# Mean of ReLU over rows: a rearranged tail, scaling on GpSimd, and a first load issued ahead of the entry barrier

## The chip, the core and the metric

The kernel runs on one core of a Trainium2 chip. The core has five engines with instruction streams of their own: TensorE (not used here), VectorE (DVE in the profile), ScalarE (ACT), GpSimd (POOL) and SyncE (SP). SyncE computes nothing; here it issues all DMA transfers. [...] The metric is the device time of one execution, in microseconds (us); smaller is better.

## The reference

```python
batch, seq, dim = 32, 512, 1024
x = np.random.randn(batch, seq, dim).astype(np.float32)

def reference(x):
    relu_x = np.maximum(x, 0)
    return np.mean(relu_x, axis=-1).astype(np.float32)
```

16384 rows of 1024 floats, 67.1 MB in all, are read once; 16384 floats (64 KB) are written.

## The kernel before, in words

The 16384 rows are laid out over 128 partitions, 128 rows to a partition (`J` = 128), so that row j of a partition is one column of a 128x128 result. The input is read in tiles of 16 rows to a partition (`NB` = 16, 8 MB), through a pool of three buffers. The first seven tiles are loaded whole, each with one DMA on SyncE's queue (L79). The last tile is loaded in pieces that get smaller (`row_pieces` 8, 4, 2, 1 rows, L86; then the sixteenth row in `col_pieces` of 512, 256 and 256 columns, L90), so that little is left to compute when the last byte lands. A load into a used buffer waits until VectorE and ScalarE are done with that buffer's rows.

A row is one instruction: it takes the maximum with zero and sums along the row into one column. Odd rows go to VectorE (`dve_row`, L20, sums in `sum_v`), even rows to ScalarE (`act_row`, L15, sums in `sum_a`). Each such instruction is followed by a short one that reads the accumulator out (`DVE_READ_ACCUMULATOR`, `ACTIVATION_READ_ACCUMULATOR`).

`finish` (L71) multiplies finished sums by 1/1024 into `res`: VectorE the odd columns (L73), ScalarE the even ones (L74). It is called twice: for the 112 columns of the first seven tiles, and for 14 columns of the last tile.

Rows 14 and 15 of the last tile are the tail (L101 to L119):

- row 14, whole: ScalarE sums its first 512 columns, VectorE its last 512; VectorE adds the halves and scales (L106);
- row 15, columns 0 to 511: ScalarE sums 256, VectorE 256;
- row 15, columns 512 to 767: VectorE; then VectorE adds the three parts so far (L111);
- row 15, columns 768 to 1023: VectorE; then VectorE adds and scales (L116);
- the store of `res` (L120) waits for L116.

Before all this stands an entry barrier of all five engines (L135 in the profile): each engine signals, GpSimd collects the signals after it has filled four constants, and releases all. The program's order on each engine is the order in which the code issues its instructions; semaphores are placed by the framework.

Of the kernel before, what the change touches and what calls it, by code (L numbers as in the profile page):

```python
# [1 line left out]

# [4 lines left out]

F32 = mybir.dt.float32
ALU = mybir.AluOpType
RELU = mybir.ActivationFunctionType.Relu  # L10


def act_row(nc, src, acc):

    nc.scalar.activation(out=src, in_=src, func=RELU, accum_out=acc)  # L15


def dve_row(nc, src, acc):

    nc.vector.tensor_scalar(  # L20
        out=src, in0=src, scalar1=0.0, scalar2=None,
        op0=ALU.max, op1=ALU.add, accum_out=acc,
    )


@with_exitstack
def kernel(
    ctx: ExitStack,
    tc: tile.TileContext,
    x: bass.AP,  # L30
    out: bass.AP,
):
    nc = tc.nc
    P = nc.NUM_PARTITIONS
    xf = x.flatten_outer_dims()
    R, D = xf.shape
    assert R % P == 0
    J = R // P
    inv = 1.0 / D
    xr = xf.rearrange("(p j) d -> p j d", p=P, j=J)  # L40
    outr = out.flatten().rearrange("(p j) -> p j", p=P, j=J)

    NB = 16
    BUFS = 3
    full = J // NB - 1

    row_pieces = []
    left = NB
    while left > 1:
        row_pieces.append(left // 2)  # L50
        left -= left // 2
    col_pieces = [D // 2, D // 4, D // 4]

    in_pool = ctx.enter_context(tc.tile_pool(name="in", bufs=BUFS))
    res_pool = ctx.enter_context(tc.tile_pool(name="res", bufs=1))
    sum_a = res_pool.tile([P, J], F32)
    sum_v = res_pool.tile([P, J], F32)
    res = res_pool.tile([P, J], F32)
    part_a = res_pool.tile([P, 2], F32)
    part_v = res_pool.tile([P, 4], F32)  # L60

    def rows(xt, lo, n, j0):

        for k in range(lo, lo + n):
            j = j0 + k
            if j % 2:
                dve_row(nc, xt[:, k, :], sum_v[:, j:j + 1])
            else:
                act_row(nc, xt[:, k, :], sum_a[:, j:j + 1])

    def finish(lo, hi):  # L71

        nc.vector.tensor_scalar_mul(out=res[:, lo + 1:hi:2], in0=sum_v[:, lo + 1:hi:2], scalar1=inv)  # L73
        nc.scalar.mul(out=res[:, lo:hi:2], in_=sum_a[:, lo:hi:2], mul=inv)  # L74

    for t in range(full):
        j0 = t * NB
        xt = in_pool.tile([P, NB, D], F32, name="xt")
        nc.sync.dma_start(out=xt, in_=xr[:, j0:j0 + NB, :])  # L79
        rows(xt, 0, NB, j0)  # L80

    j0 = full * NB
    xt = in_pool.tile([P, NB, D], F32, name="xt")
    lo = 0
    for n in row_pieces:
        nc.sync.dma_start(out=xt[:, lo:lo + n, :], in_=xr[:, j0 + lo:j0 + lo + n, :])  # L86
        lo += n
    c = 0
    for w in col_pieces:
        nc.sync.dma_start(out=xt[:, lo, c:c + w], in_=xr[:, j0 + lo, c:c + w])  # L90
        c += w

    finish(0, j0)
    lo = 0
    for n in row_pieces[:-1]:
        rows(xt, lo, n, j0)
        lo += n
    finish(j0, j0 + lo)


    last = xt[:, NB - 1, :]  # L101
    act_row(nc, xt[:, lo, :D // 2], part_a[:, 0:1])
    dve_row(nc, xt[:, lo, D // 2:], part_v[:, 0:1])
    act_row(nc, last[:, :D // 4], part_a[:, 1:2])
    dve_row(nc, last[:, D // 4:D // 2], part_v[:, 1:2])
    nc.vector.tensor_scalar(  # L106
        out=res[:, J - 2:J - 1], in0=part_a[:, 0:1], scalar1=part_v[:, 0:1], scalar2=inv,
        op0=ALU.add, op1=ALU.mult,
    )
    dve_row(nc, last[:, D // 2:3 * D // 4], part_v[:, 2:3])  # L110
    nc.vector.tensor_scalar(  # L111
        out=part_v[:, 1:2], in0=part_v[:, 1:2], scalar1=part_a[:, 1:2], scalar2=part_v[:, 2:3],
        op0=ALU.add, op1=ALU.add,
    )
    dve_row(nc, last[:, 3 * D // 4:], part_v[:, 3:4])
    nc.vector.tensor_scalar(  # L116
        out=res[:, J - 1:J], in0=part_v[:, 3:4], scalar1=part_v[:, 1:2], scalar2=inv,
        op0=ALU.add, op1=ALU.mult,
    )  # L119
    nc.sync.dma_start(out=outr, in_=res)  # L120


# [1 line left out]
_INS = ['x']  # L124
_OUTS = [((32, 512), 'float32')]


# [23 lines left out]
```

## Time and profile before

| what | us |
|---|---|
| median of 10 runs (164.80 to 165.31) | 164.93 |
| the profiled execution, its own time | 164.94 |
| span of it, first to last instruction | 163.2 |
| VectorE busy | 75.4 |
| ScalarE busy | 69.5 |
| GpSimd busy | 0.2 |
| first load issued at | 0.73 |
| store issued at | 160.74 |

Times in the profile count from the span's start. In a timeline row the columns are start, duration, engine, line, operation, tiles and shapes; what stands in square brackets is how long the engine had been idle and what released it. `SPq` is SyncE's own queue. A DMA row of the chain of waits runs from issue to landing.

### The profile page before, as it was taken

What the parts mean: (1) busy time and instruction counts of PE and PEld (TensorE: products, weight loads), DVE (VectorE), ACT (ScalarE), POOL (GpSimd) and SP (SyncE); (2) the same over time, 40 slices, a digit from 0 to 9 for tenths busy, and PEclk for the clock granted to TensorE, in tenths of its full rate; (3) what the DMA queues carried; (4) which work ended last, traced back from release to release, by engine and by line L of the source; (5) the groups of instructions that cost most, each with busy time, mean ns of one, the idle gap of its engine ahead of it and who ended that gap; (6) DMA issues with size and microseconds to landing.
All of it is one profiled execution on the core that took longest, in us unless ns stands there. A gap on an engine that the chain in (4) does not pass through costs nothing.

```text
span 163.2 us, 351 instructions
## 1 busy us (share of the span) xinstructions
DVE 75.4 (46%) x139; ACT 69.5 (43%) x133; POOL 0.2 (0%) x4
## 2 busy tenths in 40 slices
DVE  0000039800696008930099202990049700799993
ACT  3000039600694008910099002980059500797890
POOL 0000000000000000000000000000000000000000
DMA  7989998998997996996997998998999898999970
GB/s 257 514 353 418 514 418 353 514 418 353 514 450 321 514 482 289 514 482 289 514 498 325 466 482 353 450 514 370 402 514 402 370 514 353 418 442 398 412 291 16
DMA packets 2162, 67.19 MB, mean 412 GB/s; under 512 B 240, under 2 KB 624, under 8 KB 880
## 3 DMA queue, kind: packets, MB, share of 16 engines
q1 hardware_dynamic: 2160, 67.18, 96.0%
q14 instruction: 2, 0.02, 0.0%
HBM read 67.11 MB, written 0.07 MB: 412 GB/s over the span
## 4 chain that ended last, share of the span: by engine, by line
DMA 83%; DVE 14%; SPq 1%; issue 0%; DVEq 0%
DMA xt<-in_x_dram 83%; DVE xt L20 13%; SPq L86 0%; SPq L79 0%; DVE part_v L111 0%; DVE res L116 0%; DVE res L106 0%; DVE res L73 0%; DVEq L20 0%; DVEq L111 0%; DVEq L106 0%
## 5 line engine op out<-in xcount | busy, mean ns | idle before, releaser
L20 DVE TENSOR_SCALAR_CACHE_REDUCE xt<-xt 128x1024 f32<-128x1024 f32 (+1 forms) x67 | 74.4, 1172 | 85.0 <-DMA xt<-in_x_dram 84.9
L15 ACT ACTIVATE xt<-xt 128x1024 f32<-128x1024 f32 (+1 forms) x65 | 66.8, 1028 | 88.9 <-DMA xt<-in_x_dram 88.9
L15 ACT ACTIVATION_READ_ACCUMULATOR xt<-xt 128x1 f32 x65 | 12.2, 188 | 0.0
L20 DVE DVE_READ_ACCUMULATOR xt<-xt 128x1 f32 x67 | 5.6, 83 | 0.0
L15 ACT ACT_TABLE_LOAD x1 | 1.3, 1283 | 0.7 <-PEq L135 0.7
L74 ACT ACTIVATE res<-sum_a 128x56 f32<-128x56 f32 (+1 forms) x2 | 0.5, 235 | 0.1
L73 DVE TENSOR_SCALAR res<-sum_v 128x56 f32<-128x56 f32 (+1 forms) x2 | 0.4, 184 | 0.1
L111 DVE TENSOR_SCALAR part_v<-part_v,part_a 128x1 f32<-128x1 f32 x1 | 0.3, 272 | 0.1
L106 DVE TENSOR_SCALAR res<-part_a,part_v 128x1 f32<-128x1 f32 x1 | 0.2, 214 | 0.1
L116 DVE TENSOR_SCALAR res<-part_v 128x1 f32<-128x1 f32 x1 | 0.2, 215 | 0.0
L135 POOL MEMSET const-bfloat16-1.0<- 128x1 bf16 x1 | 0.1, 101 | 0.0
L135 POOL MEMSET const-uint8-127<- 128x1 uint8 x1 | 0.1, 101 | 0.0
L135 POOL MEMSET const-float32-0.0<- 128x1 f32 x1 | 0.1, 98 | 0.2 <-issue 0.2
L135 POOL MEMSET const-float32-1.0<- 128x1 f32 x1 | 0.1, 98 | 0.0
## 6 DMA issues: line engine op xcount, KB each, us to landing
xt<-in_x_dram SPq DMA_DIRECT2D x1, 4096.0 KB, 39.0
xt<-in_x_dram SPq DMA_DIRECT2D x1, 2048.0 KB, 43.5
xt<-in_x_dram SPq DMA_DIRECT2D x1, 1024.0 KB, 45.5
xt<-in_x_dram SPq DMA_DIRECT2D x1, 512.0 KB, 46.4
xt<-in_x_dram SPq DMA_DIRECT2D x1, 256.0 KB, 46.5
xt<-in_x_dram SPq DMA_DIRECT2D x2, 128.0 KB, 42.7
xt<-in_x_dram SPq DMA_DIRECT2D x7, 49.1
out_dram<-res SPq DMA_DIRECT2D x1, 64.0 KB, 1.5
```

Source lines behind the costliest of these rows:

```text
L15: nc.scalar.activation(out=src, in_=src, func=RELU, accum_out=acc)
L20: nc.vector.tensor_scalar(out=src, in0=src, scalar1=0.0, scalar2=None, op0=ALU.max, op1=ALU.add, accum_out=acc,)
L73: nc.vector.tensor_scalar_mul(out=res[:, lo + 1:hi:2], in0=sum_v[:, lo + 1:hi:2], scalar1=inv)
L74: nc.scalar.mul(out=res[:, lo:hi:2], in_=sum_a[:, lo:hi:2], mul=inv)
L106: nc.vector.tensor_scalar(out=res[:, J - 2:J - 1], in0=part_a[:, 0:1], scalar1=part_v[:, 0:1], scalar2=inv, op0=ALU.add, op1=ALU.mult,)
L111: nc.vector.tensor_scalar(out=part_v[:, 1:2], in0=part_v[:, 1:2], scalar1=part_a[:, 1:2], scalar2=part_v[:, 2:3], op0=ALU.add, op1=ALU.add,)
L116: nc.vector.tensor_scalar(out=res[:, J - 1:J], in0=part_v[:, 3:4], scalar1=part_v[:, 1:2], scalar2=inv, op0=ALU.add, op1=ALU.mult,)
L135: nc = _bacc.Bacc("TRN2", target_bir_lowering=False, num_devices=1)
```

## The change

Five things are done.

1. All sums go to one tile `sums`. `finish` becomes one GpSimd instruction over all columns, odd and even, in place of one on VectorE and one on ScalarE.
2. Row 14's halves are added and scaled on GpSimd.
3. Row 15: ScalarE also takes 128 of the columns 512 to 767, VectorE the other 128. VectorE's instructions for row 15 start from the sum of the one before (`init`, an operand in SBUF), so that no add is needed between them. GpSimd scales ScalarE's first part; ScalarE multiplies its second part by 1/1024 and adds that; VectorE's last instruction scales its running sum and adds ScalarE's.
4. The store waits for VectorE and for GpSimd's third instruction.
5. After the program has been compiled, its first load (the first tile, 8 MB) is taken out of the body and put ahead of SyncE's drain in the entry barrier. The other loads stay behind the barrier.

The built program differs in one more instruction: at the start of GpSimd's body, behind the barrier, stands a request to load a library of GpSimd instructions, which the program before does not have.

```diff
-def dve_row(nc, src, acc):
+def dve_row(nc, src, acc, init=None):
     nc.vector.tensor_scalar(
-        out=src, in0=src, scalar1=0.0, scalar2=None,
+        out=src, in0=src, scalar1=0.0, scalar2=init,
         op0=ALU.max, op1=ALU.add, accum_out=acc,
     )
+def issue_ahead_of_entry_barrier(nc):
+    entry, body = nc.cur_f.blocks[0].instructions, None
...
+    first = body[load]
...
+    del body[load]
+    at = next(k for k, i in enumerate(entry) if i.engine == first.engine and i.opcode == "Drain")
+    entry.insert(at, first)
...
     def finish(lo, hi):
-        nc.vector.tensor_scalar_mul(out=res[:, lo + 1:hi:2], in0=sum_v[:, lo + 1:hi:2], scalar1=inv)
-        nc.scalar.mul(out=res[:, lo:hi:2], in_=sum_a[:, lo:hi:2], mul=inv)
+        nc.gpsimd.tensor_scalar(
+            out=res[:, lo:hi], in0=sums[:, lo:hi], scalar1=inv, scalar2=0.0, op0=ALU.mult, op1=ALU.add,
+        )
...
-    act_row(nc, xt[:, lo, :D // 2], part_a[:, 0:1])
-    dve_row(nc, xt[:, lo, D // 2:], part_v[:, 0:1])
-    act_row(nc, last[:, :D // 4], part_a[:, 1:2])
-    dve_row(nc, last[:, D // 4:D // 2], part_v[:, 1:2])
-    nc.vector.tensor_scalar(
-        out=res[:, J - 2:J - 1], in0=part_a[:, 0:1], scalar1=part_v[:, 0:1], scalar2=inv,
-        op0=ALU.add, op1=ALU.mult,
+    act_row(nc, prev[:, :512], part[:, 0:1])
+    dve_row(nc, prev[:, 512:], part[:, 1:2])
+    nc.gpsimd.tensor_scalar(
+        out=res[:, J - 2:J - 1], in0=part[:, 0:1], scalar1=part[:, 1:2], scalar2=inv, op0=ALU.add, op1=ALU.mult,
     )
-    dve_row(nc, last[:, D // 2:3 * D // 4], part_v[:, 2:3])
-    nc.vector.tensor_scalar(
-        out=part_v[:, 1:2], in0=part_v[:, 1:2], scalar1=part_a[:, 1:2], scalar2=part_v[:, 2:3],
-        op0=ALU.add, op1=ALU.add,
+    act_row(nc, last[:, :256], part[:, 2:3])
+    dve_row(nc, last[:, 256:512], part[:, 3:4])
+    nc.gpsimd.tensor_scalar(
+        out=part[:, 4:5], in0=part[:, 2:3], scalar1=inv, scalar2=0.0, op0=ALU.mult, op1=ALU.add,
     )
-    dve_row(nc, last[:, 3 * D // 4:], part_v[:, 3:4])
-    nc.vector.tensor_scalar(
-        out=res[:, J - 1:J], in0=part_v[:, 3:4], scalar1=part_v[:, 1:2], scalar2=inv,
-        op0=ALU.add, op1=ALU.mult,
+    act_row(nc, last[:, 512:640], part[:, 5:6])
+    dve_row(nc, last[:, 640:768], part[:, 6:7], init=part[:, 3:4])
+    nc.scalar.activation(
+        out=part[:, 7:8], in_=part[:, 5:6], func=ACT.Identity, scale=inv, bias=part[:, 4:5],
+    )
+    dve_row(nc, last[:, 768:], part[:, 8:9], init=part[:, 6:7])
+    nc.vector.scalar_tensor_tensor(
+        out=res[:, J - 1:J], in0=part[:, 8:9], scalar=inv, in1=part[:, 7:8], op0=ALU.mult, op1=ALU.add,
     )
     nc.sync.dma_start(out=outr, in_=res)
+    pools.close()
+    tc.close()
+    tc.compile()
+    issue_ahead_of_entry_barrier(nc)
```

## The prediction

> **What bounds the kernel now.** I read the page first: the busy shares, the slices, the DMA queue and the chain that ended last.
>
> ```profile
> span 163.2 us, 351 instructions
> DVE 75.4 (46%) x139; ACT 69.5 (43%) x133; POOL 0.2 (0%) x4
> ...
> q1 hardware_dynamic: 2160, 67.18, 96.0%
> HBM read 67.11 MB, written 0.07 MB: 412 GB/s over the span
> ...
> DMA 83%; DVE 14%; SPq 1%; issue 0%; DVEq 0%
> ```
>
> Both computing engines are idle more than half the time, while the load queue keeps 16 DMA engines busy 96% of the span. The chain is DMA for 83%. So the middle of the kernel is the stream of loads, and there are two ends that are not: the time until the stream starts, and the time from its last byte to the store. The timeline shows both. First the start:
>
> ```profile
> 0.33 0.10 POOL L135 MEMSET const-uint8-127<- 128x1 uint8 x1
> 0.72 1.28 ACT L15 ACT_TABLE_LOAD   x1 [0.72 <-PEq L135]
> 0.73 0.36 SPq L79 DMA_DIRECT2D xt<-in_x_dram  x1
> ```
>
> SyncE's own first instruction, its drain in the entry barrier, starts the span at 0.00. Its first load is issued at 0.73: the reader is to see 0.73 us in which SyncE only waits for the barrier. The first packet moves at 1.72, about 1.0 us after the issue. Then the tail:
>
> ```profile
> 157.98 0.63 ACT L15 ACTIVATE xt<-xt 128x512 f32<-128x512 f32 x1
> 158.03 0.68 DVE L20 TENSOR_SCALAR_CACHE_REDUCE xt<-xt 128x512 f32<-128x512 f32 x1
> ...
> 158.82 0.21 DVE L106 TENSOR_SCALAR res<-part_a,part_v 128x1 f32<-128x1 f32 x1
> 158.95 0.19 ACT L15 ACTIVATION_READ_ACCUMULATOR xt<-xt 128x1 f32 x1
> 158.95 0.41 DVE L20 TENSOR_SCALAR_CACHE_REDUCE xt<-xt 128x256 f32<-128x256 f32 x1
> ...
> 159.63 0.08 DVE L20 DVE_READ_ACCUMULATOR xt<-xt 128x1 f32 x1
> 159.82 0.27 DVE L111 TENSOR_SCALAR part_v<-part_v,part_a 128x1 f32<-128x1 f32 x1
> 160.01 0.41 DVE L20 TENSOR_SCALAR_CACHE_REDUCE xt<-xt 128x256 f32<-128x256 f32 x1
> 160.34 0.08 DVE L20 DVE_READ_ACCUMULATOR xt<-xt 128x1 f32 x1
> 160.46 0.21 DVE L116 TENSOR_SCALAR res<-part_v 128x1 f32<-128x1 f32 x1
> 160.74 0.35 SPq L120 DMA_DIRECT2D out_dram<-res  x1
> ```
>
> The semaphore updates in the trace give the landings of the last loads: row 14 at 157.96, then row 15's 512 columns at 158.60, 256 at 158.94, 256 at 159.26. VectorE has its last 256 columns in hand at 159.26 but begins on them at 160.01, since three small instructions (L106, L111, L116) stand between its sums. ScalarE is done at 159.14. The store is issued 160.74 − 157.96 = 2.78 us after row 14 lands. All below is counted from that landing, which I call L.
>
> **Part 1, the first load moves.** SyncE then issues it at about 0.00 instead of 0.73. It passes SyncE's drain and its barrier signal, nothing of another queue: the two other first loads stay behind the barrier. One issue takes 0.36 (this row), so SyncE's signal comes at about 0.40 instead of 0.01. The barrier is closed by GpSimd, which is drained at 0.48 and looks at the signals at 0.53, so 0.13 us is left and the release does not move. If it moved, the second load (1.14 now) and the activation table would be late, and both have the 22 us until the first tile lands as cover. Behind the first load the stream never runs dry: later loads were issued 39 to 60 us ahead of their landing. So the whole stream and with it L comes 0.73 us earlier. Bounds: 0 (the time to the first packet is set by something else that is late) to 0.73; I take 0.73, because the 1.0 us from issue to first packet has nothing of the barrier in it.
>
> **Part 2, `finish` on GpSimd.** VectorE loses 0.19 and 0.17 (L73), ScalarE 0.26 and 0.21 (L74). The first pair, at 148.1 to 149.1, is followed by waits for a DMA of 0.97 and 0.25 us: worth nothing. Of the second pair only 0.03 to 0.05 shows, as VectorE starts row 14 at 158.03 and ScalarE at 157.98, 0.02 after L.
>
> **Part 3, the tail on VectorE, from L.** Row 14's 512 columns: start 0.02, sum read out 0.69 later (158.03 to 158.72): 0.71. Row 15's 256 columns land at 0.64, and L106 no longer stands before them: start 0.66, read out 0.42 later (160.01 to 160.43): 1.08. Then 128 columns with a running sum. No row has that length: 256 take 0.41 and 512 take 0.68, so 1.05 ns a column and 0.14 fixed, which gives 0.28. The initial value from SBUF I price by the small rows, 0.21 with one such operand (L116) against 0.17 with none (L73): 0.04, bounds 0 to 0.10 (L111 with two operands takes 0.27). It waits for its own predecessor, and the gap to L116, which waits so, is 0.04. So 1.08 + 0.04 + 0.28 + 0.04 + 0.01 = 1.45. The last 256 columns, landed at 1.30, are not waited for: 1.45 + 0.04 + 0.41 + 0.04 + 0.01 = 1.95. The final instruction waits for VectorE and ScalarE, as L111 did, which began 0.11 after the read-out: start 2.06, duration between L116's 0.21 and L111's 0.27, I take 0.24: 2.30. The store follows 0.06 later, as now: 2.36. That is 2.78 − 2.36 = 0.42 us less.
>
> **Part 4, the tail on ScalarE.** 512 columns are read out at 0.75, 256 at 1.18 (0.66 + 0.52, the present rows), and 128 start at 1.09; by its rows (0.63 and 0.42) 128 take 0.31, read out at 1.50. The scaling ACTIVATE waits for GpSimd's last instruction and takes 0.21, as L74's did on 7 columns. If GpSimd is in time it ends at 1.61 + 0.21 = 1.82, before VectorE needs it (2.06).
>
> **Part 5, GpSimd: the price not in the trace.** Its four instructions are strictly in order. Call x the time of one small one, signal to signal. The 14-column one starts at 0.05 (after row 13). Row 14's waits for both halves: 0.85. The scaling of ScalarE's part waits for 1.18 + 0.04 = 1.22 and for the two ahead of it. It ends at 1.22 + x up to x = 0.37, at 0.85 + 2x up to 0.80, at 0.05 + 3x beyond. ScalarE's ACTIVATE and the hand-over add 0.05 + 0.21 + 0.04 = 0.30, and VectorE needs it at 2.06. So GpSimd costs nothing up to x = 0.455; at 0.6 it costs 0.29; at 0.65 nearly all of Part 3 is gone; at 0.95 all of the change.
>
> What is x? Nearest row of this engine: MEMSET of one column, 0.10, with no read in it; that is the lower end. The nearest row of the operation is L106 on VectorE, 0.21. Against the move stands the Trainium skill, "GPSIMD Engine Reference", Performance versus the Vector engine: GpSimd is the wrong place for elementwise work, 1.96 times slower on a two-input add. By row alone the chain of GpSimd ends at 1.43 and hides; by the rule, as an estimate, x = 0.21 × 1.96 = 0.42, it ends at 1.69 and still hides, by 0.07. I take 0.42, with 0.10 and 0.65 as ends: tail gain 0.42 to 0.03.
>
> The 112-column instruction comes at about 148, with 9 us to the tail. It is also the first after the library load, and the same page (Instruction dispatch) has a first call to a freshly loaded kernel cost about 6 us more with nothing to show in a profile: 9 covers 6, and no row here can say. Without that cover the tail's GpSimd chain would be late by what is over.
>
> **The sum.** Span 163.2 − 0.73 − 0.42 = 162.05. Outside the span lie 164.94 − 163.2 = 1.74 us, unchanged. 164.94 − 1.15 = 163.79; the profiled execution stands 0.01 over the median, so 163.8.
>
> **Rivals.**
>
> *GpSimd ends last* (x between 0.46 and 0.95): for it, three instructions in a row stand ahead of ScalarE's last step. Against it, even the page's factor leaves x below the limit. At x = 0.6: 163.79 + 0.29 = 164.1; at 0.8: 164.5. From x = 1.06 the kernel is measurably slower.
>
> *The library load takes DMA time: slower.* It stands where the stream has no room, at 0.7 us, with queues 96% full. Bytes on the 16 engines cost 1 us per 0.41 MB (412 GB/s) if spread evenly, and on one engine alone 1 us per 27 KB (a 64 KB packet takes 2.42 us in the trace). The present instruction queue moves 0.02 MB in the span. Lower end 0; upper, as an estimate from the 128 KiB of instruction memory in each of eight cores (same page, Specifications), 1.05 MB / 412 GB/s = 2.5 us. It decides from 1.15 + 0.33 = 1.48 us on, that is 0.6 MB evenly spread or 40 KB on one engine. Against it: whether those bytes pass through these engines at all no row shows, and the spread of the last landings over the engines (158.25 to 159.26) can hide up to 1 us on an early one. At 2.5 us: 166.3.
>
> *The head does not move*: the first packet comes when it came, and only the tail counts: 164.94 − 0.42 = 164.5. Against it stands that SyncE is idle from 0.01 to 0.65.
>
> **How the numbers follow.** As summed 0.62 (163.5 to 164.1); GpSimd last 0.11; library traffic 0.17; head unmoved 0.05; x above 1.06 0.05. What a measurement of this kernel can tell from no change is about 0.2%, 0.33 us: 164.6 to 165.26. Faster: 0.62, 0.09 of GpSimd, 0.05, 0.02 of the library: 0.78. Same: 0.02 and 0.04. Slower: 0.11 of the library and 0.05. The range 163.4 to 165.1 leaves out the slower cases and little below: Part 3 has at most 0.2 us more to give.
>
> **What would show it.** Right: first load at 0.0 and barrier release still near 0.65; the landings of the last four loads earlier by 0.73 each; VectorE's last three instructions 0.04 to 0.11 apart, none waiting for ACT; the store 2.36 after L. Wrong: the final VectorE instruction released by ScalarE, and that by GpSimd; an instruction-queue row of tenths of a MB and landings that moved by less than 0.73; a barrier that waits for SyncE.

## The result

The changed kernel takes 163.83 us (median of 9 runs, 163.63 to 164.10) against 164.96 us for the kernel before beside it: a ratio of 0.9931, interval 0.9923 to 0.9940, or 1.13 us less. Measured twice more beside the kernel before, it was 0.99 us (163.98 against 164.97) and 1.17 us (163.69 against 164.86) faster. The profiled execution took 163.96 us with a span of 162.18 us, so 1.78 us lie outside the span, as many as before (164.94 less 163.16).

The page of the changed kernel, the lines that answer to those of before:

```profile
span 162.2 us, 358 instructions
DVE 74.7 (46%) x135; ACT 69.7 (43%) x134; POOL 1.2 (1%) x8
...
q1 hardware_dynamic: 2160, 67.18, 96.7%
q14 instruction: 2, 0.02, 0.0%
HBM read 67.11 MB, written 0.07 MB: 414 GB/s over the span
...
DMA 84%; DVE 13%; SPq 1%; issue 0%; DVEq 0%
```

The middle is as it was: the same packets, one point more of the chain in DMA. GpSimd works 1.2 us instead of 0.2. The timeline of its start (start, duration, engine, line, operation):

```profile
0.00 2.01 SPq L92 DMA_DIRECT2D xt<-in_x_dram  x3
...
0.78 1.28 ACT L15 ACT_TABLE_LOAD   x1 [0.78 <-PEq L155]
```

The first row joins the first three loads. The first of them now goes at 0.00 instead of 0.73, the second, behind the barrier, at 0.78; the first packet moves at 1.01 instead of 1.72. The activation table, which shows when the barrier is released, comes 0.05 later (0.777 against 0.723). Then the timeline of the tail. Row 14 landed at 157.41: that is the time at which the trace has the load's last update of its semaphore, the counter on which an engine waits for a load or for another engine.

```profile
157.43 0.69 DVE L20 TENSOR_SCALAR_CACHE_REDUCE xt<-xt 128x512 f32<-128x512 f32 x1
157.51 0.22 POOL L85 TENSOR_SCALAR res<-sums 128x14 f32<-128x14 f32 x1 [8.70 <-DVE xt L20]
...
158.06 0.42 DVE L20 TENSOR_SCALAR_CACHE_REDUCE xt<-xt 128x256 f32<-128x256 f32 x1
...
158.30 0.26 POOL L118 TENSOR_SCALAR res<-part 128x1 f32<-128x1 f32 x1 [0.57 <-ACT xt L15]
158.38 0.19 ACT L15 ACTIVATION_READ_ACCUMULATOR xt<-xt 128x1 f32 x1
...
158.52 0.35 DVE L20 TENSOR_SCALAR_CACHE_REDUCE xt<-xt,part 128x128 f32<-128x128 f32 x1
158.65 0.19 POOL L123 TENSOR_SCALAR part<-part 128x1 f32<-128x1 f32 x1
158.67 0.19 ACT L15 ACTIVATION_READ_ACCUMULATOR xt<-xt 128x1 f32 x1
158.79 0.08 DVE L20 DVE_READ_ACCUMULATOR xt<-xt,part 128x1 f32 x1
158.91 0.48 DVE L20 TENSOR_SCALAR_CACHE_REDUCE xt<-xt,part 128x256 f32<-128x256 f32 x1
158.95 0.30 ACT L128 ACTIVATE part<-part 128x1 f32<-128x1 f32 x1
159.31 0.08 DVE L20 DVE_READ_ACCUMULATOR xt<-xt,part 128x1 f32 x1
159.51 0.16 DVE L132 SCALAR_TENSOR_TENSOR res<-part 128x1 f32<-128x1 f32 x1
159.73 0.35 SPq L135 DMA_DIRECT2D out_dram<-res  x1
```

No row of VectorE or ScalarE from 157.43 on names another engine in brackets. A bracket stands only at more than 0.15 us of idle, so the shorter gaps are read from the ends of the rows: ScalarE's step (L128) begins at 158.95, behind its own read-out, which ends at 158.86, and GpSimd's last instruction had ended at 158.84; VectorE's last one (L132) begins at 159.51, behind its own read-out at 159.40, and ScalarE's step had ended at 159.25. Neither waits for GpSimd. The store goes 2.32 us after row 14's landing instead of 2.78.

### The profile page after: what moved, and what is told of

The parts are those of the page before. It is cut to its first block, busy times and chain, and to the rows that moved or that the text cites. A ratio compares the mean times of both kernels' runs of the same rounds, so it can differ in the third digit from the quotient of the medians.

```text
span 162.2 us, 358 instructions
## 1 busy us (share of the span) xinstructions
DVE 74.7 (46%) x135; ACT 69.7 (43%) x134; POOL 1.2 (1%) x8
## 4 chain that ended last, share of the span: by engine, by line
DMA 84%; DVE 13%; SPq 1%; issue 0%; DVEq 0%
DMA xt<-in_x_dram 84%; DVE xt L20 13%; SPq L100 1%; DVE res L132 0%; DVEq L20 0%; SPq L92 0%; DVEq L132 0%
## 5 line engine op out<-in xcount | busy, mean ns | idle before, releaser
L20 DVE TENSOR_SCALAR_CACHE_REDUCE xt<-xt 128x1024 f32<-128x1024 f32 (+1 forms) x65 | 73.6, 1195 | 84.7 <-DMA xt<-in_x_dram 84.4
L85 POOL TENSOR_SCALAR res<-sums 128x112 f32<-128x112 f32 (+1 forms) x2 | 0.5, 252 | 156.8 <-DVE xt L20 156.8
L20 DVE TENSOR_SCALAR_CACHE_REDUCE xt<-xt,part 128x128 f32<-128x128 f32 (+1 forms) x2 | 0.8, 412 | 0.1
L128 ACT ACTIVATE part<-part 128x1 f32<-128x1 f32 x1 | 0.3, 297 | 0.1
L132 DVE SCALAR_TENSOR_TENSOR res<-part 128x1 f32<-128x1 f32 x1 | 0.2, 159 | 0.1
```

The costliest lines, as they stand in the source:

```text
L20: nc.vector.tensor_scalar(out=src, in0=src, scalar1=0.0, scalar2=init, op0=ALU.max, op1=ALU.add, accum_out=acc,)
L85: nc.gpsimd.tensor_scalar(out=res[:, lo:hi], in0=sums[:, lo:hi], scalar1=inv, scalar2=0.0, op0=ALU.mult, op1=ALU.add,)
L128: nc.scalar.activation(out=part[:, 7:8], in_=part[:, 5:6], func=ACT.Identity, scale=inv, bias=part[:, 4:5],)
L132: nc.vector.scalar_tensor_tensor(out=res[:, J - 1:J], in0=part[:, 8:9], scalar=inv, in1=part[:, 7:8], op0=ALU.mult, op1=ALU.add,)
```

## The experiments

Each ran beside the kernel before on its own chip; the experiments used three chips, and rows with the same figure in the third column ran on the same one. "L" is row 14's landing in the profiled execution, "tail" the time from L to the store, both from the trace.

| kernel | median us | before beside it | L | tail |
|---|---|---|---|---|
| before | 164.93 | – | 157.96 | 2.78 |
| changed | 163.83 | 164.96 | 157.41 | 2.32 |
| head only | 164.28 | 164.97 | 157.24 | 2.79 |
| tail only | 164.49 | 164.97 | 157.94 | 2.33 |
| scalings on GpSimd only | 165.19 | 164.97 | 158.04 | 2.74 |
| changed, second time | 163.98 | 164.97 | 157.60 | 2.34 |
| head and library load | 164.17 | 165.04 | 157.10 | 2.77 |
| one more on GpSimd | 163.79 | 165.04 | 157.41 | 2.33 |
| four more on GpSimd | 164.10 | 165.04 | 157.79 | 2.61 |
| three loads ahead | 163.71 | 164.86 | 157.14 | 2.33 |
| changed, third time | 163.69 | 164.86 | 157.04 | 2.34 |
| two sums, last piece 192 | 163.59 | 165.04 | 157.17 | 2.23 |
| the same, second time | 163.66 | 164.86 | 157.21 | 2.23 |
| two sums, last piece 256 | 163.92 | 164.86 | 157.24 | 2.29 |

### The two halves apart

Head only: the kernel before, with the changed kernel's function behind it.

```diff
...
     nc.sync.dma_start(out=outr, in_=res)
...
+    pools.close()
+    tc.close()
+    tc.compile()
+    issue_ahead_of_entry_barrier(nc)
```

> The kernel before with the first load ahead of the barrier alone. If the two parts simply add, the time falls by the head's share: 0.73 us by the prediction (first packet 0.71 us earlier in the changed kernel's trace), 0.56 us if what the last landings of that one trace show (158.70 instead of 159.26) is what remains: 164.2 to 164.4. Rival: the head's gain needs the new tail to show, since a tail of small instructions takes it up: less than 0.3 us.

Measured: 164.28 against 164.97, ratio 0.9960 (0.9946 to 0.9974), 0.69 us less. In its trace the first packet moves at 1.01 and row 14 lands at 157.24: 0.72 us earlier at both ends of the stream, with the old tail unchanged at 2.79. The head's gain does not need the new tail.

Tail only: the changed kernel without the move.

```diff
     tc.compile()
-    issue_ahead_of_entry_barrier(nc)
```

> The changed kernel with its first load behind the barrier, as before: the tail's share alone. Additive theory: 0.42 to 0.46 us less than before, 164.5; the landings stand where they stood before, the store 2.3 us after row 14's landing. Rival: the library load that GpSimd now makes takes DMA time, which in the changed kernel ate into the head: then landings later than before by 0.1 to 0.2 us and a gain of only 0.25 to 0.35 us.

Measured: 164.49 against 164.97, ratio 0.9971 (0.9961 to 0.9982), 0.48 us less. Row 14 landed at 157.94, 0.02 from where it was, and the tail is 2.33. So no landing was late in this trace, although this kernel loads the GpSimd library. The halves add within what can be told: 0.69 + 0.48 = 1.17, where the whole measured 0.99 on the same chip (0.81 to 1.30 by its interval), and 1.13 and 1.17 in its other two measurements.

### The library load

The scalings alone moved to GpSimd, in the kernel before:

```diff
-    sum_a = res_pool.tile([P, J], F32)
-    sum_v = res_pool.tile([P, J], F32)
+    sums = res_pool.tile([P, J], F32)
+    sum_a = sum_v = sums
...
     def finish(lo, hi):
-        nc.vector.tensor_scalar_mul(out=res[:, lo + 1:hi:2], in0=sum_v[:, lo + 1:hi:2], scalar1=inv)
-        nc.scalar.mul(out=res[:, lo:hi:2], in_=sum_a[:, lo:hi:2], mul=inv)
+        nc.gpsimd.tensor_scalar(
+            out=res[:, lo:hi], in0=sums[:, lo:hi], scalar1=inv, scalar2=0.0, op0=ALU.mult, op1=ALU.add,
+        )
```

> The kernel before with the two scalings on GpSimd, tail and head untouched; it also makes the library load. If the load costs no DMA time and the scalings were hidden, no difference to before beyond 0.05 us either way. If the library load passes through the 16 DMA engines, the last landing is late and the time up by what it costs (0.15 us would explain the changed kernel's head).

Measured: 165.19 against 164.97, ratio 1.001 (1.000 to 1.0021): slower by more than the 0.05 expected, at the edge of what can be told from nothing. Its trace has the tail 0.04 shorter, as Part 2 of the prediction had it, and row 14 0.08 later. One more kernel was made for it: head only, with one GpSimd instruction whose result is not used.

```diff
+    spare = res_pool.tile([P, 1], F32)
...
+    nc.gpsimd.tensor_scalar(
+        out=spare, in0=sum_a[:, 0:1], scalar1=inv, scalar2=0.0, op0=ALU.mult, op1=ALU.add,
+    )
     finish(0, j0)
```

> The kernel before with the first load moved (as in head_only), and one GpSimd tensor_scalar on one column whose result is not used, so that the library load is made and nothing else changes. Library free: head_only's 164.28 within 0.1 us. Library takes DMA time: later landings and up to 0.25 us more, 164.4 to 164.5, which would explain that the kernel with the two scalings on GpSimd measured 165.19 against 164.97, and that head and tail alone (0.69 and 0.48) give 0.05 to 0.15 us more than the changed kernel has.

Measured: 164.17 against 165.04, ratio 0.9954 (0.9941 to 0.9966); head only had 0.9960. Row 14 landed at 157.10, earlier than in head only. The load is made: its trace has two `MODIFY_POOL_CONFIG` at 0.8 us, as the changed kernel's has, which this row shows.

```profile
L85 POOLq MODIFY_POOL_CONFIG  x2: 11/11/11, 0.8 to 0.8; - x2
```

The instruction queue's row is 2 packets and 0.02 MB in the pages of the changed kernel and of this one, as it was before. The library load costs no time that this kernel and tail only can see; the 0.22 us of the kernel with the scalings alone has no cause that its trace shows, and stays open.

### The changed kernel again

> The changed kernel once more beside its parts on the same chip: 1.1 us less than before; a second trace for the landings. If the head's shortfall in the first trace (0.56 of 0.71 us at the last landing) was chance in the DMA stream, this trace shows another number; if it belongs to the change, the same within 0.05 us.

> The changed kernel beside the two other tails, on the same chip: 163.8 to 164.0. Its row 14 landed at 157.41 and 157.60 in two traces, while five other traces with the moved load lie between 157.2 and 157.8: if that is scatter of the stream, a third trace falls anywhere in that span.

Measured: 163.98 and 163.69. Row 14 landed at 157.60 and 157.04; the tail was 2.34 in both. Over the eleven traces with the moved load it landed between 157.04 and 157.79, 157.30 in the mean; over the three without it between 157.94 and 158.04, 157.98 in the mean. The means are 0.68 apart. One and the same kernel, the changed one, landed row 14 anywhere within 0.56 us in its three traces, so the first trace's 0.55 instead of 0.73 lies within the scatter of the stream.

### How much room GpSimd has

One more, and four more, small instructions with unused results stand ahead of the one that ScalarE's last step waits for; the tile `part` gets six more columns for them. With four:

```diff
...
+    for k in range(4):
+        nc.gpsimd.tensor_scalar(
+            out=part[:, 10 + k:11 + k], in0=part[:, 2:3], scalar1=inv, scalar2=0.0, op0=ALU.mult, op1=ALU.add,
+        )
     nc.gpsimd.tensor_scalar(
         out=part[:, 4:5], in0=part[:, 2:3], scalar1=inv, scalar2=0.0, op0=ALU.mult, op1=ALU.add,
     )
```

> The changed kernel with one more small GpSimd instruction (result not used) ahead of the one that ScalarE's last step waits for. By its trace GpSimd ended at 158.84 and could have ended at about 159.11 before VectorE's last instruction waits, 0.27 us of room; one more costs about 0.22 us: no difference, 163.8 to 164.0. If the room is what the prediction had for x = 0.42 (0.07), 0.15 us more.

> As before with four more. If one costs 0.22 us: 4 x 0.22 less 0.27 us of room, 0.6 us later, 164.5, VectorE's last instruction released by ScalarE. If small GpSimd instructions overlap as the four constants at the start do (0.03 us apart): no difference. If each costs the prediction's 0.42: 1.4 us later, 165.2.

Measured: 163.79 with one, 164.10 with four. One is hidden: ScalarE's step waits for it, and VectorE still reaches its last instruction as late after L as in the changed kernel (2.10), the tail staying at 2.33.

```profile
159.03 0.29 ACT L132 ACTIVATE part<-part 128x1 f32<-128x1 f32 x1 [0.16 <-POOL part L127]
```

The timeline of the kernel with four:

```profile
158.77 0.19 ACT L15 ACTIVATION_READ_ACCUMULATOR xt<-xt 128x1 f32 x1
...
159.03 0.63 POOL L124 TENSOR_SCALAR part<-part 128x1 f32<-128x1 f32 x4
...
159.62 0.19 POOL L127 TENSOR_SCALAR part<-part 128x1 f32<-128x1 f32 x1
159.70 0.08 DVE L20 DVE_READ_ACCUMULATOR xt<-xt,part 128x1 f32 x1
159.85 0.29 ACT L132 ACTIVATE part<-part 128x1 f32<-128x1 f32 x1 [0.60 <-POOL part L127]
160.17 0.16 DVE L136 SCALAR_TENSOR_TENSOR res<-part 128x1 f32<-128x1 f32 x1 [0.39 <-ACT part L132]
160.40 0.35 SPq L139 DMA_DIRECT2D out_dram<-res  x1
```

Here the brackets name the rival's chain: VectorE released by ScalarE after 0.39 idle, ScalarE by GpSimd after 0.60. Five starts lie between 159.03 and 159.62, so 0.15 us apart, less than the 0.22 expected. The tail grew by 2.61 − 2.33 = 0.28 us, and 4 x 0.15 = 0.60, so 0.32 us of room were there. The medians of the two kernels are 0.31 us apart on the same chip, but with four runs each, spread over 0.37 and 0.69 us, they could not tell it alone.

### The barrier made later

```diff
-    issue_ahead_of_entry_barrier(nc)
+    for _ in range(3):
+        issue_ahead_of_entry_barrier(nc)
```

> The changed kernel with all three first loads ahead of SyncE's drain instead of one. Three issues take 0.38 + 0.43 + 0.43 us and the drain 0.13 behind them, so the barrier is released near 1.6 instead of 0.7 us, and the activation table is loaded that much later. If the barrier has the 22 us to the first landing as cover, no difference to the changed kernel (163.8 to 164.0). If the release matters to anything that sets the end, up to 0.9 us more.

Measured: 163.71, with the changed kernel at 163.69 beside it. Its start:

```profile
0.00 1.31 SPq L92 DMA_DIRECT2D xt<-in_x_dram  x3
...
1.71 1.28 ACT L15 ACT_TABLE_LOAD   x1 [1.71 <-PEq L156]
```

The release and the table are 0.93 us later than in the changed kernel, and the time is the same: the 22 us to the first tile's landing do cover them.

### Another tail

By the trace of the changed kernel VectorE begins its last 256 columns at 158.91, 0.21 after they landed, and one ScalarE and one GpSimd step hang on the sums. A tail with two sums for row 15 does without them. It stands in place of the changed kernel's instructions for row 15; with 192 columns last:

```diff
-    col_pieces = [512, 256, 256]
+    col_pieces = [512, 320, 192]
...
+    dve_row(nc, last[:, :384], part[:, 3:4])
+    act_row(nc, last[:, 384:832], part[:, 5:6])
+    dve_row(nc, last[:, 832:], part[:, 6:7], init=part[:, 3:4])
+    nc.vector.tensor_scalar(
+        out=res[:, J - 1:J], in0=part[:, 6:7], scalar1=part[:, 5:6], scalar2=inv, op0=ALU.add, op1=ALU.mult,
+    )
     nc.sync.dma_start(out=outr, in_=res)
```

> The changed kernel with another tail for row 15: pieces of 512, 320 and 192 columns; VectorE sums 384 and, running on, the last 192; ScalarE sums the 448 between; one VectorE instruction adds and scales, with no GpSimd or ScalarE step behind it. By the prediction's durations VectorE begins the last 192 columns when they land (1.31 us after row 14), reads out at 1.71, ends at 2.03 and the store goes at 2.09 instead of 2.32: 0.23 us less than the changed kernel, 163.6. Rival: smaller pieces land later or ScalarE's 448 columns end last: no gain.

> The tail with pieces of 512, 320 and 192 columns and two sums, once more beside the changed kernel: 0.2 us less by the tail (store 2.2 after row 14's landing instead of 2.33), that is 0.1 to 0.3 us less in the median. If the first measurement (163.59) was a good draw of the stream, no difference.

> The same two-sum tail with the changed kernel's pieces of 512, 256 and 256: VectorE sums columns 0 to 255 and the last 256, ScalarE the 512 between. By the durations VectorE starts the last 256 at 1.31 after row 14's landing, reads out at 1.79, ends at 2.12, store at 2.18 to 2.2: 0.13 us less than the changed kernel. If the smaller last piece is what helps, no gain here.

Measured: 163.59 and 163.66 with 192 columns last, 163.92 with 256 (VectorE sums columns 0 to 255 and the last 256, ScalarE the 512 between). In the traces the tail is 2.23 and 2.29, so 0.10 and 0.04 us shorter than the changed kernel's, not 0.23 and 0.13 to 0.15. The timeline of the second run with 192 shows the missing tenth; the last piece landed at 158.51:

```profile
158.62 0.41 DVE L20 TENSOR_SCALAR_CACHE_REDUCE xt<-xt,part 128x192 f32<-128x192 f32 x1 [0.18 <-DMA xt<-in_x_dram]
158.84 0.19 ACT L15 ACTIVATION_READ_ACCUMULATOR xt<-xt 128x1 f32 x1
158.96 0.08 DVE L20 DVE_READ_ACCUMULATOR xt<-xt,part 128x1 f32 x1
159.16 0.21 DVE L124 TENSOR_SCALAR res<-part 128x1 f32<-128x1 f32 x1
```

The instruction waits for two semaphores: VectorE's own sum, and, in a wait instruction of its own ahead of it, the landing. It began 0.12 after the landing (158.624 against 158.507; 0.12 in the two other traces of this tail as well), where one that waits for the landing alone, as row 14's does, began 0.02 after it. Beside the changed kernel (163.69) neither the 163.66 nor the 163.92 is a difference that can be told, since the intervals of the ratios overlap; the shorter tail is shown in the traces alone.

## Why the prediction was right, step by step

Predicted 163.8, measured 163.83; predicted span 162.05, the trace's 162.18. The steps hold, as shown below; that the figure comes within 0.03 is luck, as the same kernel measured 163.98 and 163.69 the other times. The prediction's 1.74 outside the span comes from a rounded span (163.2 for 163.16); the traces have 1.78 before and after, and the rounding cancels in the sum. Its steps against the runs:

**Part 1, the head: right, with one detail wrong.** 0.73 us was taken; the first packet came 0.71 earlier, row 14 in the mean of the traces 0.68, and head only gave 0.69. The sign that the last four landings come 0.73 earlier was not met in the first trace, which has 0.55 to 0.57 for them; only the mean over the traces comes near it. The release of the barrier was to stay: it moved by 0.05. SyncE's drain, its first instruction in the entry barrier, took 7 ns before; directly behind a DMA issue it takes 131 ns. The first row is of the kernel before, the second of the changed one.

```profile
L135 SPq DRAIN  x1: 7/7/7, 0.0 to 0.0; - x1
L155 SPq DRAIN  x1: 131/131/131, 0.4 to 0.4; - x1
```

It ends at 0.56, so the 0.13 us that the prediction had left were more than used up. Nothing was late for it, as the kernel with three loads ahead shows with 0.93.

**Part 2, the scalings: right in the trace, not shown in the time.** The pair at 148 is worth nothing, and VectorE and ScalarE begin row 14 at 157.43, 0.02 after L; with the scalings alone on GpSimd the tail is 0.04 shorter, within the 0.03 to 0.05 predicted. The median of that kernel went the other way, 0.22 up, and why stays open.

**Part 3, VectorE's tail: right in sum, with two sizes off that cancel.** The read-outs came at 0.71, 1.07, 1.46 and 1.98 after L; predicted were 0.71, 1.08, 1.45 and 1.95. The running sum costs 0.06 to 0.07 for each instruction (0.48 against 0.42 in this trace and 0.41 before, on 256 columns), not 0.04; the last instruction took 0.16, not 0.24. Store at 2.32 instead of 2.36; tail only gave 0.48 where 0.42 was predicted. Where the tail's 0.46 comes from can be read in the two timelines: VectorE begins its last 256 columns at 1.50 after L instead of 2.05, which gives 0.55; the running sum takes 0.07 of it back, and the last instruction starts 0.11 instead of 0.04 after the read-out but is 0.06 shorter. Which of the moved or merged steps gives how much of the 0.55 was not measured one by one.

**Part 4, ScalarE: right by its margin.** The scaling ACTIVATE took 0.30, not the 0.21 of L74's row. It takes its offset from SBUF, and that row has none; that this is the cause is not shown, since no run parts it from what else differs. It ended at 1.84, predicted 1.82, as it started 0.07 before the predicted time.

**Part 5, GpSimd: right that it hides; x too large.** 0.42 was taken, from 0.21 by the factor of the Trainium skill's "GPSIMD Engine Reference", Performance versus the Vector engine, which is measured there on an add of two inputs over 2048 columns and was carried over to one column. From ScalarE's read-out (158.57) to GpSimd's end (158.84) are 0.27 us, and the two-operand instruction took 0.26 against VectorE's 0.21. The measurement decides: on one column the ratio was 1.2, not 1.96. The end at 1.43 is the one that the prediction gave "by row alone", to the hundredth by chance: the read-out came 0.02 sooner, and the step took 0.27 instead of 0.21 and 0.04 of hand-over. The room was 0.3 us instead of 0.07. The predicted time would have been the same with any x up to 0.455, so the median does not test x; the trace does. On the first call after a library load (same page, Instruction dispatch, about 6 us), no run here shows that cost: the first GpSimd instruction, 148 us after the load, began 0.17 after VectorE's read-out and took 0.28, and the second, which can't be a first call, began 0.16 after its own. In the kernel with the head and the library load the first one comes already 22.6 us after the load, and is as short as the last one of the changed kernel (192 ns; both begin 0.07 after ScalarE's signal).

```profile
L114 POOL TENSOR_SCALAR spare<-sum_a 128x1 f32<-128x1 f32 x1 | 0.2, 192 | 23.0 <-ACT xt L15 23.0
```

What a first call costs sooner after the load, no run tests.

**The rivals.** GpSimd last: not the case here, but shown by the kernel with four more to be the next limit of this tail. The library's DMA time: not seen in head only with the load, nor in the landing of tail only; the 0.22 us of the scalings alone are not explained by it. The head that does not move: excluded by head only.

## What to carry to other kernels

Where a stream of loads sets the middle, look at both ends of it: what the issuing engine waits for before the first load, and how many small dependent instructions follow the last landing; the two gains add. When such small steps are moved to an idle engine, add up its queue in order and compare its end with the moment the result is needed: here 0.3 us of room took one more instruction of 0.15 us without cost and not four. A tail that is shorter by a tenth in the trace can vanish in the median, when the stream ahead of it lands anywhere within 0.75 us.

## What the runs showed of the hardware that was not expected

- SyncE's drain in the entry barrier took 125 to 131 ns directly behind a DMA issue (eleven traces), and 7 ns without one ahead of it (three traces).
- The same stream of loads, started at the same time (first packet at 0.99 to 1.01), landed row 14 anywhere from 157.04 to 157.79 in eleven traces.
- One-column GpSimd instructions with nothing to wait for follow one another every 0.15 us, though each is listed with 0.19.
- Where a VectorE instruction waits for two semaphores, the traces show a separate wait instruction ahead of it for one of them. Where that one came last, it started later: 0.12 us after the semaphore's update for the last 192 columns, 0.10 for the changed kernel's last VectorE instruction, 0.09 to 0.15 over all traces. Where its own came clearly last, or it had only one, it was 0.02.
